# Encoder block on eight cores: the gating unit's mixing moved into the next FFN, attention with longer lags, constants, staging loads and final multiply re-timed

## The chip, the cores and the metric

The kernel runs on the 8 cores of one Trainium2 chip, each core with one of 8 sequences. The time is the device time of the slowest core in microseconds (us). Some executions fall in a slow state, in which one die, sometimes both, runs at a lower granted clock (the share of full speed that the throttle gave the matmul engine) and takes some per cent longer, whatever the kernel is.

## The reference, cut to what matters

```python
x = x + 0.5 * swiglu(rmsnorm(x, norm_ffn1), w_gate, w_up, w_down)     # FFN 1
h = rmsnorm(x, norm_mix)
z = h @ w_in                      # q, k, v | u, v_s | two gates
y_att = chunked_rel_attention(q, k, v, rel_bias)     # 64-frame chunks, 9-chunk key band, 8 heads
y_sgu = spatial_gating(gelu(z_sgu), ...)             # layer norm, 128x128 mixing per group, times u
merged = g_att * (y_att @ w_branch_att) + g_sgu * (y_sgu @ w_branch_sgu)
x = x + merged @ w_out
x = x + 0.5 * swiglu(rmsnorm(x, norm_ffn2), ...)     # FFN 2
return rmsnorm(x, norm_final)
```

Per core x is 4096 x 1024, the FFN width is 2816.

## The kernel before

A sequence is worked in 8 tiles of 512 frames. For tile t the order on the matmul engine (PE) is: FFN 1 of tile t+1 with attention of tile t interleaved, merge and output projection of tile t, input projections of tile t+1 ("win"), FFN 2 of tile t. Engines run their instructions in program order, and a helper adds the semaphore waits. Weights come through six slots of 1 MB. At first use a chunk is loaded as float32 and cast by a software DMA issued from POOL; some uses later it is written back as bfloat16, and from then on loaded by a plain DMA from SP.

An FFN is a generator of 60 "pieces": 44 gate and up pieces of 8 matmuls, then 16 down pieces of 11. `hooks` maps a piece to work that is put behind it.

```python
for f2 in range(NFC // 2):                       # 11 weight chunks
    sl, k = get_slot(("ffs", i, f2))
    for a in range(2):
        ...  # 8 matmuls into bank bg; ACT: tanh or silu -> TG; (tanh: DVE multiplies by bank bg)
        hook(); yield
        ...  # 8 matmuls into bank bu; DVE: HT[fc] = bank bu * TG   (L469)
        if a == 1: free_slot(k)                  # allows the load of the chunk six ahead
        hook(); yield
```

The start, as DVE and the POOL queue see it (cut):

```python
...  # sp: G3, then GF, BG, LNG, LNB, BSB; pool: IDB, then six weight chunks; act: X of tile 0
p.add("dve", memset NHALF, QBD, VR, PB)
... # four norms of tile 0
def late_consts():
    p.dma("pool", RB); p.dma("pool", WST)        # behind the six chunks in the same queue
    p.add("dve", memset of part of WST)          # waits for the WST load   (L346)
    p.add("dve", BG *= 0.5)
```

The mixing at the end of the projections, and one attention step:

```python
for s in range(4):                               # sgu_mix, in banks 4 and 5
    b = 4 + s % 2
    ...  # 8 small matmuls (L603); DVE: + BSB -> TG (L608), * UT -> YS
# attention: scores(i) | transp(i-1) | pv(i-2), 34 steps
def scores(i):
    ...  # PE scores; DVE add bias, row minimum; ACT exp
    p.add("dve", reciprocal of the row sum)      # waits for ACT   (L662)
    p.add("dve", probabilities *= reciprocal)    # (L664)
```

The norms and the final norm:

```python
def norm_stats(t, which, s):
    if which == 0 and t >= 2: p.dma("sp", XS[s % 2] <- x)
    p.add("act", square with row sum); rsqrt on POOL
    p.add("act", XN = x * rsqrt)                 # waits for POOL
def final(t, s):
    p.add("act", square with row sum); rsqrt on POOL
    p.add("dve", X = X * rsqrt * GF)             # waits for POOL   (L773)
```

## Time and profile before

| | before |
|---|---|
| time, median of the first 3 runs | 3028.04 us (3026.66 to 3031.44) |
| span of the slowest core in the profile | 3025.5 us |
| PE busy | 2854.2 us, so 171 us idle |
| first FFN matmul, first projection matmul | 27.1 us, 192.1 us |
| FFN 2 of tile 0 from, to | 467.5 us, 589.6 us |

A line of a wait table reads "who <- who ended it: us in total, times, longest". A timeline line reads "start, duration, engine, line, operation, out<-in, count, [idle before <- releaser]". In the slices every digit is the busy share of 1/40 of the span in tenths. In a table by stage each engine (PE, its weight load PEld, DVE, ACT, POOL, in this order) has its busy time and number of instructions; the last three columns are granted PE clock, DMA share (busy share of the 16 DMA engines; it can read a little over 1) and GB/s. The lines on which the argument stands are in the prediction below. An attention start in the timeline of the kernel before:

```profile
1338.31 1.28 ACT L658 ACT_TABLE_LOAD   x1 [3.38 <-DVE ASTAT L651]
1341.36 0.69 PE L674 MATMUL ps<-IDB,PB 128*128 128x128 bf16 x5 [2.58 <-DVE PB L664]
```

PE reaches the transposition of the first probabilities before they are scaled and stands 2.58 us.

### The profile page before, as it was taken

Reading aid. Unit: us, or ns where it says so; the run is one execution under the profiler, and the core shown is the slowest. Engines: PE = TensorE matmul, PEld = TensorE weight load, DVE = VectorE, ACT = ScalarE, POOL = GpSimd, SP = SyncE. Lnnn points to the kernel's source line nnn. Section 1 sums busy time; section 2 is a strip of 40 time slices with the busy share of each in tenths; the row PEclk is TensorE's granted clock in tenths of the full one; section 3 lists DMA queues with packets and bytes.
Section 4 is the critical chain, followed back from the end, with each engine's and each line's share of the span. In section 5 each row is a group of like instructions: output and inputs, shape, how many; then the busy total and the mean of one; then the engine's idle time right before and its main releaser. Section 6 shows DMA issues by size and latency. Waiting matters only on the chain.

```text
span 3025.5 us, 44880 instructions; the slowest of 8 cores (3003.3 to 3025.5 us)
## 1 busy us (share of the span) xinstructions
PE 2854.2 (94%) x15680; PEld 1387.6 (46%) x15680; DVE 1271.2 (42%) x2457; ACT 1017.5 (34%) x1784; POOL 181.5 (6%) x424
## 2 busy tenths in 40 slices
PE   2999999999989999999999999999999999999998
PEld 1444444455434554445544454444544445445444
DVE  1236443364423644246441464425544255456322
ACT  1223332244312443224332243323433244434221
POOL 1110111100100001000000000000000000000000
PEclk7999999999999999999999999999999999999999
DMA  9987799876876446754344444345343452433432
GB/s 202 170 179 168 142 202 198 201 216 143 220 163 198 164 120 201 194 181 161 133 140 162 156 143 148 131 160 167 132 154 140 157 193 100 163 114 104 167 139 91
DMA packets 103436, 485.37 MB, mean 160 GB/s; under 512 B 9008, under 2 KB 9520, under 8 KB 85936
## 3 DMA queue, kind: packets, MB, share of 16 engines
q1 hardware_dynamic: 82352, 384.35, 36.8%
q0 software_dynamic: 20288, 96.05, 19.7%
q8 instruction: 131, 2.15, 0.3%
q10 hardware_dynamic: 576, 2.10, 0.2%
q14 instruction: 89, 0.73, 0.1%
HBM read 513.50 MB, written 65.01 MB: 191 GB/s over the span
## 4 chain that ended last, share of the span: by engine, by line
PE 79%; DVE 6%; DMA 5%; issue 4%; ACT 2%; another core or an unknown queue 2%; POOL 1%; DVEq 0%; ACTq 0%; POOLq 0%; SPq 0%
PE ps L486 18%; PE ps L448 17%; PE ps L465 17%; PE ps L716 7%; PE ps L523 4%; PE ps L727 4%; PE ps L748 3%; PE ps L509 2%; DMA XS<-x 2%; PE ps L674 2%; PE ps L686 2%; PE ps L413 1%; POOL STAT L369 1%; DVE SC L651 1%
## 5 line engine op out<-in xcount | busy, mean ns | idle before, releaser
L465 PE MATMUL ps<-XT,SLOT 128*128 128x512 bf16 x2816 | 681.0, 386 | 38.6 <-DVE HT L469 38.6
L448 PE MATMUL ps<-XT,SLOT 128*128 128x512 bf16 x2816 | 685.6, 388 | 14.9 <-ACT TG L459 11.7
L486 PE MATMUL ps<-SLOT,HT 128*128 128x512 bf16 x2816 | 636.0, 380 | 2.2 <-DMA SLOT<-wd 2.2
L469 DVE TENSOR_TENSOR HT<-ps,TG 128x512 bf16<-128x512 f32 x352 | 242.0, 690 | 511.3 <-PE ps L465 417.9
L465 PEld LDWEIGHTS ps<-XT,SLOT 128*128 128x128 bf16 x2816 | 271.7, 99 | 348.2 <-issue 61.4
L448 PEld LDWEIGHTS ps<-XT,SLOT 128*128 128x128 bf16 x2816 | 274.4, 99 | 329.8 <-issue 44.8
L486 PEld LDWEIGHTS ps<-SLOT,HT 128*128 128x128 bf16 x2816 | 270.4, 98 | 301.5 <-issue 4.3
L658 ACT ACTIVATE PB<-SC,ASTAT 128x576 bf16<-128x576 f32 (+7 forms) x256 | 190.4, 744 | 478.1 <-DVE ASTAT L651 478.0
L459 ACT ACTIVATE TG<-ps 128x512 f32<-128x512 f32 x176 | 103.7, 594 | 420.8 <-PE ps L448 420.8
L716 PE MATMUL ps<-XT,SLOT 128*128 128x512 bf16 x1024 | 243.6, 381 | 0.0
L651 DVE CUSTOM_DVE_ANT_0 SC<-ps,RB 128x576 f32<-128x576 f32 (+7 forms) x256 | 182.3, 712 | 30.9 <-PE ps L646 28.8
L492 DVE SCALAR_TENSOR_TENSOR X<-ps,X 128x512 f32<-128x512 f32 x128 | 88.4, 690 | 220.2 <-PE ps L486 216.9
L677 ACT ACTIVATE PTS<-ps 128x640 bf16<-128x640 bf16 (+4 forms) x256 | 167.4, 654 | 28.6 <-PE ps L674 27.7
L662 DVE RECIPROCAL ASTAT<-ASTAT 128x1 f32<-128x1 f32 x256 | 41.9, 164 | 315.1 <-ACT PB L658 315.1
L509 PE MATMUL ps<-XT,SLOT 128*128 128x512 bf16 x768 | 168.4, 379 | 0.0
L721 ACT ACTIVATE TG<-ps,BG 128x512 f32<-128x512 f32 x128 | 87.1, 686 | 232.8 <-PE ps L716 232.8
L417 DVE TENSOR_TENSOR XT<-ps,G 128x1024 bf16<-128x1024 bf16 x96 | 116.8, 1219 | 114.0 <-PE ps L413 114.0
L731 DVE SCALAR_TENSOR_TENSOR TG<-TG,ps 128x512 f32<-128x512 f32 x128 | 87.4, 687 | 178.8 <-PE ps L727 150.0
L716 PEld LDWEIGHTS ps<-XT,SLOT 128*128 128x128 bf16 x1024 | 99.1, 98 | 113.6 <-issue 2.4
L455 DVE SCALAR_TENSOR_TENSOR TG<-TG,ps 128x512 f32<-128x512 f32 x176 | 120.6, 685 | 48.0 <-ACT TG L453 40.7
L367 POOL TENSOR_SCALAR STAT<-STAT 128x1 f32<-128x1 f32 x128 | 24.3, 189 | 1825.0 <-ACT XN L397 1392.5
L674 PE MATMUL ps<-IDB,PB 128*128 128x128 bf16 x1200 | 109.4, 220 | 25.6 <-DVE PB L664 24.4
(73 smaller groups left out, 2352.5 us busy)
## 6 DMA issues: line engine op xcount, KB each, us to landing
SLOT<-ffs SPq DMA_DIRECT2D x133, 1024.0 KB, 5.7
SLOT<-wds SPq DMA_DIRECT2D x48, 1024.0 KB, 4.9
SLOT<-fsrc POOLq DMA_DIRECT2D x43, 1024.0 KB, 13.2
SLOT<-mgs SPq DMA_DIRECT2D x47, 768.0 KB, 5.4
SLOT<-wis SPq DMA_DIRECT2D x31, 1024.0 KB, 5.8
ffs<-SLOT SPq DMA_DIRECT2D x22, 1024.0 KB, 10.0
SLOT<-wds SPq DMA_DIRECT2D x24, 768.0 KB, 4.7
SLOT<-wd POOLq DMA_DIRECT2D x16, 1024.0 KB, 14.1
```

Of the source, the lines that this page charges most:

```text
L448: p.add("pe", lambda e, kc=kc, W=W, bg=bg: e.matmul(bank(bg), lhsT=W[:, kc * 128:(kc + 1) * 128], rhs=xt[:, kc, :], start=(kc == 0), stop= ...
L465: p.add("pe", lambda e, kc=kc, W=W, bu=bu: e.matmul(bank(bu), lhsT=W[:, 1024 + kc * 128:1024 + (kc + 1) * 128], rhs=xt[:, kc, :], start=(k ...
L469: p.add("dve", lambda e, buf=buf, bu=bu, fc=fc: e.tensor_tensor(out=HT[:, fc, :], in0=bank(bu), in1=buf[:], op=ALU.mult), reads=[rb(bu), b ...
L486: p.add("pe", lambda e, fc=fc, W=W, by=by, s=s: e.matmul(bank(by), lhsT=HT[:, fc, s * 128:(s + 1) * 128], rhs=W, start=(fc == 0), stop=(fc ...
L509: p.add("pe", lambda e, kc=kc, W=W, b=b, cc=cc: e.matmul(bank(b), lhsT=W[:, kc * 512 + cc * 128:kc * 512 + (cc + 1) * 128], rhs=XT[t % 2][ ...
L523: p.add("pe", lambda e, kc=kc, W=W, b=b, s=s: e.matmul(bank(b), lhsT=XT[t % 2][:, kc, s * 128:(s + 1) * 128], rhs=W[:, kc * 512:(kc + 1) * ...
L651: p.add("dve", lambda e: e.tensor_tensor_reduce(out=sc[:, 0:nb], in0=S2[:, 512 - n_prev * 64:512 + n_cur * 64], in1=RB[:, hp, j0:576], sca ...
L658: p.add("act", lambda e: e.activation(out=pbuf[:, off + j0:off + 576], in_=sc[:, 0:nb], func=AF.Exp, bias=ASTAT[:, a0:a0 + 1], scale=-1.0, ...
L674: p.add("pe", lambda e, kt=kt: e.transpose(out=pt[:, kt * 128:(kt + 1) * 128], in_=pbuf[:, kt * 128:(kt + 1) * 128], identity=IDB[:]), rea ...
L677: p.add("act", lambda e: e.activation(out=PTS[i % 2][:, kt0 * 128:640], in_=pt[:, kt0 * 128:640], func=AF.Copy), reads=[rb(6)], writes=[(" ...
L716: p.add("pe", lambda e, kc=kc, W=W, bgt=bgt, j=j: e.matmul(bank(bgt), lhsT=W[:, j * 1024 + kc * 128:j * 1024 + (kc + 1) * 128], rhs=XT[par ...
L727: p.add("pe", lambda e, c4=c4, W=W, bbr=bbr, j=j, Y=Y: e.matmul(bank(bbr), lhsT=W[:, 2048 + j * 512 + c4 * 128:2048 + j * 512 + (c4 + 1) * ...
```

## The change

The intent is to fill PE's gaps. The core of the diff:

```diff
-            p.dma("sp", G3); p.dma("pool", IDB)          # ahead of X
+            p.dma("act", TG[0] <- ident); p.dma("act", G3)   # behind X (now half on sp); DVE casts the identity
-            (memsets of QBD, VR, PB and the WST memset at the front of DVE)
+            add_hook(hk, 6, const_loads)                 # pieces of the first FFN
+            add_hook(hk, 40, const_ops)
...
-                for f2 in range(NFC // 2):
+                for f2 in (3, 8, 9, 10, 2, 0, 1, 4, 5, 6, 7):
...
-                (mixing behind the projections, banks 4 and 5)
+            def sgu_hooks(hk, t):
+                for s in range(4):
+                    add_hook(hk, 3 + 3 * s, P(sgu_mix, t, s))   # in the next FFN, bank = dense_bank()
...
-            N_ATT = 3 * 34
+            N_ATT = 4 * 35
-                    for fn, i in ((scores, step), (transp, step - 1), (pv, step - 2)):
+                    for fn, i in ((scores, step), (normal, step - 1), (transp, step - 2), (pv, step - 3)):
...
-            norm_stats: XS load, square, root, scaling in one place
+            norm_sq, norm_cp: the scaling some pieces after the square (on DVE at the start, behind the first FFN and in the last merge)
+                    add_hook(hk, 12, P(load_xs, t + 2, 0), P(load_xs, t + 2, 1))
+            (XS of s = 2, 3 loaded right behind the scaling of s = 0, 1)
...
+                    if s:
+                        add_hook(hk, down(1, s), P(final_mul, t, s - 1))   # one step after the root
```

The new order of chunks keeps the parts of HT that hold the mixing's operands (0 to 3 and 8 to 15) unwritten until the fourth piece of mixing is done.

## The prediction

> **What bounds the kernel now.** I read the page's busy shares and 40 slices first, then who waited for whom on the matmul engine, then the timeline around its long gaps, and last the engines' shares by stage.
>
> ```profile
> PE 2854.2 (94%) x15680; PEld 1387.6 (46%) x15680; DVE 1271.2 (42%) x2457; ACT 1017.5 (34%) x1784; POOL 181.5 (6%) x424
> PE   2999999999989999999999999999999999999998
> DMA  9987799876876446754344444345343452433432
> q1 hardware_dynamic: 82352, 384.35, 36.8%
> q0 software_dynamic: 20288, 96.05, 19.7%
> ```
>
> PE is the bound in all but the first slice; DVE and ACT are far from full. The work of PE doesn't change, so only its idle time (3025.5 - 2854.2 = 171 us) and time at a low clock can be won. DMA is near full in the early slices. Per MB of destination, the casting software queue costs 0.197 x 3025.5 / 96.05 = 6.2 us and the hardware queue 0.368 x 3025.5 / 384.35 = 2.9 us.
>
> ```profile
> PE ps L603 <- DVE TG L608: 39.1, 16, 4.2
> PE ps L465 <- DVE HT L469: 38.6, 1, 38.6
> PE ps L674 <- DVE PB L664: 24.4, 26, 2.9
> PE ps L413 <- ACT XN L402: 17.9, 7, 4.9
> PE ps L448 <- ACT TG L459: 11.7, 4, 8.0
> ```
>
> Two waits dominate: the gating unit's mixing (L603), 4.9 us in each of 8 tiles, and one single wait of 38.6 us at the start. The timeline says what that one is:
>
> ```profile
> 75.90 0.48 DVE L346 MEMSET WST<- 64x512 bf16 x1 [48.94 <-DMA WST<-wst]
> 76.48 1.28 DVE L469 TENSOR_TENSOR HT<-ps,TG 128x512 bf16<-128x512 f32 x2
> 77.31 3.47 PE ps L465 x8
> ```
>
> (The third line is from the chain of work that ended last.) DVE runs in order. The memset of WST waits for a load behind six weight chunks in the same queue, and the evictions that PE needs stand behind it.
>
> The low clock comes with the gaps. After a mixing stage:
>
> ```profile
> 1211.34 0.64 PE L603 MATMUL ps<-WST,HT 128*64 128x128 bf16 x8 [4.19 <-DVE TG L608]
> 1213.37 3.59 PE L448 MATMUL ps<-XT,SLOT 128*128 128x512 bf16 x8
> 1218.70 1.89 PE L448 MATMUL ps<-XT,SLOT 128*128 128x512 bf16 x8
> ```
>
> Eight matmuls take 3.59 us instead of 1.89. Summing all start-to-start times of 512-column matmuls between 0.3 and 0.5 us, less the usual 0.216, gives 43 us: 16 after the eight mixing stages, 11 after six attention starts, the rest at the start, at the end and after DMA waits.
>
> ```profile
> 27.00:39.00 12.00, 11.57 (x40) 4.50 (x40) 0.00 (x0) 1.42 (x3) 0.00 (x0) 1.00 1.03 234
> 39.00:77.00 38.00, 0.00 (x0) 0.00 (x0) 1.09 (x3) 0.37 (x1) 0.70 (x1) 0.55 1.03 197
> 77.00:146.00 69.00, 68.69 (x311) 30.82 (x312) 13.90 (x21) 18.09 (x29) 7.86 (x15) 0.97 0.91 169
> 235.00:372.00 137.00, 136.04 (x752) 66.18 (x752) 70.75 (x201) 53.37 (x133) 10.52 (x21) 0.98 0.76 162
> 467.00:583.00 116.00, 112.70 (x538) 51.67 (x539) 28.51 (x38) 25.34 (x39) 11.75 (x24) 0.97 1.02 210
> ```
>
> The last two columns are DMA share and GB/s. DMA is full while PE stands still at 39 to 77 us, and full again in the second half of the first tile.
>
> **What the Trainium skill says.** "TensorE: Matmul & The Clock Gate", section "What's actually happening": an idle window of about 3.4 us puts the array back to half clock and a similar busy window brings it back. The trace agrees: gaps of 3.9 us and more are followed by 8 to 14 matmuls 0.43 us apart; gaps of about 1 us are not. "DMA: Bandwidth & Descriptors", section "Issuing engines are not separate DMA queues": loads issued from several engines share the same 16 DMA engines. The share of 1.03 in 27 to 77 us with three issuers agrees; moving X and the constants between queues buys order, not bandwidth. "ScalarE: Activation LUTs", section "What ACT_TABLE_LOAD costs": about 1283 ns per load; the trace has 1.28 us.
>
> **The change part by part.**
>
> (a) Start. Memsets and constants leave the front; the wait on WST leaves DVE (memsets at piece 40 of the first FFN), so PE's 38.6 us plus 1.6 us of low clock go. The four norms are pipelined, with their scaling on DVE; the first matmul should move from 27 to about 20 us, another 7 us. But those 47 us aren't free: DMA was full in that time. The work that must land before the first FFN is done: 11 gate/up chunks x 6.5 us (1.05 MB x 6.2) = 72; down weights 4 x 6.5 + 2 x 4.9 = 36; X for two tiles, 4.2 MB x 2.9 = 12; constants about 9; six write-backs x 3 = 18. Sum about 147 us. The last down chunk then lands at about 149 to 158 us instead of 160, and from it some 16 us of matmuls remain: the first FFN ends at 165 to 175 us instead of 187.5. Gain 18 us of the 47; the rest turns into waits for weights. The memsets at piece 40 (3.47 + 3.47 + 2.62 us and two small ones, 10 us of DVE) may cost 2 us, hidden in the same waits.
>
> (b) Mixing in pieces in the next FFN. The 32 small matmuls per tile stay, but each group of 8 stands among dense ones, with a dense bank. Per tile the two gaps (about 3.9 + 1.0 us) and about 2 us of low clock go: 7 us. This needs the new order of weight chunks, so that HT 0..3 and 8..15 are still whole; that costs nothing. For tiles 2 to 6 this is 5 x 7 = 35 us. Tiles 0 and 7 start an FFN with attention beside it, so the layer norm chain (DVE ends it about 4 us after the last projection matmul) delays the first score evictions and about half of the gain stays a wait: 3 to 4 us each. Tile 1's gain falls into the full-DMA stage at 467 to 583 us, where a weight wait of 2.25 us is already seen: 1 us.
>
> (c) Attention with one more step between exp and transposition. The reciprocal no longer blocks DVE (315 us of DVE idle before L662), but PE lost only 24 us to this, most of it as one gap per tile at the start of each FFN with attention: 0.66 + 2.58 us, plus about 1.9 us of low clock. At that place DVE still does the last tile's final multiply, ACT still loads the exp table (1.28 us), and the next tanh stands behind the first exp, so, replayed with the durations of the start at 1332 us, the second score eviction ends at about 1342.2 us while PE wants those banks for the third scores at 1339.9. By this working 2.5 us of gap stay in place of 3.2 and the low clock shrinks: 1.5 us x 6 = 9 us. The small gaps elsewhere in attention (ten of 0.3 to 0.6, and 0.73, 1.39, 1.27) go: 7 us.
>
> (d) Staging loads. ACT waited 118.6 us for XS; PE lost 8.01 + 0.98 + 1.09 + 1.60 us = 11.7 to it and 1.6 to the low clock. XS now loads at least 6 pieces (10 us) ahead against landings of 5.5 to 10 us in later tiles and 20 us in tile 1: 12.5 us.
>
> (e) Final multiply one step later. It takes a 2.5 us wait from DVE 32 times; PE sees it before the last merge (3.55 us, and 2.7 of low clock): 5 us. The drain at the end, last matmul to last store, stays at about 17 us. The norm gaps at 187.5 and 2895 us (3.8 and 4.8 us) keep their chain of eviction, square, root, scaling and transposition, so stay.
>
> Sum: 18 (a) + 35 + 4 + 4 + 1 (b) + 9 + 7 (c) + 12.5 (d) + 5 (e) = 95.5 us. 3028 - 96 = 2932 us.
>
> **The rivals.** First: the start is not DMA-limited and the whole 47 us comes through. For it: PE waits for no weight in the first 500 us of the trace. Against: at 39 to 77 us DMA share is 1.03 with PE idle, and each chunk lands about 9.5 us after the one before, against 6.9 us of matmuls. It would give about 2905. Second: attention's first gap vanishes as intended, 31 us instead of 9: about 2910; both together 2880. Third: the added pieces make DVE late where attention runs (DVE 70.75 of 137 us there), mixing adds 1.4 us of DVE per piece, banks come free late, and gaps of a microsecond appear at each piece; or ACT or POOL wait in order for a norm and stop the FFN as in (d). Shares near one half speak against it; it would give 2960 or so. Fourth: early tiles, with DMA full, return nothing: (a) and the first tiles' (b) fall to 5 us, 2950.
>
> **Range and chances.** 2932 us, 8 in 10 between 2890 and 2962. The threshold of 2% is at 2967.5, a gain of 60.5 us. The parts that rest on plain removal of a seen gap ((b) for tiles 2 to 6, (d), (e) and the small gaps: 35 + 12.5 + 5 + 7 = 59.5) reach it almost alone. Faster 0.91, within 2% 0.08, slower 0.01.
>
> **What would show it.** (a) The wait for L469 gone, waits of L448 or L486 for DMA of SLOT in the first 180 us in its place, the first FFN ending at 165 to 175 us. (b) No wait at the mixing matmuls over 1 us, no run of 0.43 us matmuls at the start of FFN 2 in tiles 2 to 6, a period per tile of some 358 instead of 368 us. (c) At each attention start a wait of scores for the eviction before them, about 2 us. (d) ACT's wait for XS near zero. The prediction is wrong if PE's idle time stays over 120 us, if the first FFN ends before 155 or after 185 us, or if new waits for DVE or ACT appear in every tile.

## The result, and the profile after

The two fast runs of the changed kernel took 2917.69 and 2916.78 us; two more runs fell in the slow state (2969 and 3158 us). The ratio of the fast runs is 0.9632, 95% interval 0.9604 to 0.966: 3.7% faster. A ratio is the mean time of one kernel's fast runs over that of the other's in the same rounds, so it isn't quite the ratio of the medians. Experiments compare with 2917 us, the middle of the two.

The page of the changed kernel, its slowest core with a span of 2916.1 us:

```profile
PE 2825.4 (97%) x15680; PEld 1381.4 (47%) x15680; DVE 1265.9 (43%) x2470; ACT 1005.9 (34%) x1772; POOL 181.0 (6%) x423
PE   6799999899999999999999999999999999999998
```

PE's idle time fell from 171 to 91 us, and its busy time by 29 us with the same number of matmuls. The latter is low clock: the start-to-start times of 512-column matmuls between 0.3 and 0.5 us, less 0.216 each, sum to 26 us instead of 43; these sums don't explain the other 12 us (the ends of matmuls are modelled). Slices 1 and 2, where PE had stood still, read 6 and 7 instead of 2 and 9. Who PE waited for now (line numbers shift with every edit: L603, L642, L465 and L486 of the kernel before are L622, L661, L483 and L504 here):

```profile
PE ps L430 <- DVE XN L417: 33.1, 8, 19.2
PE ps L661 <- DVE ASTAT L685: 15.4, 8, 2.1
PE ps L504 <- DMA SLOT<-wd: 12.3, 4, 6.0
PE ps L466 <- DMA SLOT<-fsrc: 12.2, 2, 11.8
```

The mixing's 39.1 us and the 38.6 us at the start are gone. In place of the second stand waits for weights, one of them 11.8 us long (at 82.7 us). L430 is the norms' transposition, L661 the score matmuls of an attention start (the third scores at six of them, 2.13 us each).

Where the time came from, by the first matmul of a stage in both traces:

| stage begins | before, us | after, us | earlier by, us |
|---|---|---|---|
| FFN 1 of tile 0, up | 27.1 | 32.3 | -5.1 |
| its down matmuls | 146.2 | 124.7 | 21.5 |
| projections of tile 0 | 192.1 | 177.1 | 15.0 |
| FFN 1 of tile 1 | 235.6 | 213.9 | 21.6 |
| FFN 2 of tile 0 | 467.5 | 439.4 | 28.1 |
| FFN 1 of tile 2 | 589.6 | 570.2 | 19.4 |
| FFN 1 of tile 3 | 965.3 | 925.4 | 39.9 |
| FFN 1 of tile 6 | 2068.5 | 1991.3 | 77.2 |
| FFN 2 of tile 7, up | 2900.8 | 2792.3 | 108.5 |
| end | 3025.5 | 2916.1 | 109.4 |

Tile 0's up matmuls win 26.6 us (from -5.1 to 21.5), and the stages with the first two mixings 6.6 and 6.5, but 15 us are lost again by 570 us: 6.5 in the first down matmuls and 8.7 in FFN 2 of tile 0. From then on each tile is 11 to 21 us shorter. The table by stage of the changed kernel shows what holds the early part:

```profile
32.30:124.70 92.40, 80.19 (x352) 35.11 (x353) 17.97 (x23) 20.17 (x32) 9.44 (x17) 0.93 1.03 191
124.70:177.10 52.40, 45.40 (x241) 21.48 (x240) 23.24 (x26) 5.99 (x11) 7.53 (x17) 0.91 1.00 181
439.00:570.00 131.00, 122.47 (x595) 55.31 (x594) 35.18 (x49) 27.23 (x42) 15.50 (x31) 0.95 0.97 197
```

DMA is full (1.03, 1.00, 0.97) in all three stages in which PE waits for weights; the second and the third give time back, the first wins less than the 38.6 us of its old wait. But a full DMA alone isn't a loss: its share was 1.00 from 177 to 214 us and from 345 to 439 us too, where PE was busy for 37.0 of 37 and 93.7 of 94 us. The share says where waits can come; the wait table says whether they do.

A piece of mixing among dense matmuls, and the front, in the timeline of the changed kernel:

```profile
1170.19 0.41 PE L622 MATMUL ps<-WST,HT 128*64 128x128 bf16 x8
1170.54 1.90 PE L466 MATMUL ps<-XT,SLOT 128*128 128x512 bf16 x8
...
18.11 0.23 DVE L328 CAST IDB<-TG 128x128 bf16<-128x128 f32 x1 [16.92 <-DMA TG<-ident]
21.43 1.22 DVE L434 TENSOR_TENSOR XT<-ps,G 128x1024 bf16<-128x1024 bf16 x1 [2.33 <-DMA G<-g]
32.25 3.21 PE L466 MATMUL ps<-XT,SLOT 128*128 128x512 bf16 x8 [1.48 <-DVE XT L434]
```

The eight small matmuls cost 0.35 us from start to start of the neighbours, and the next eight run at 1.90 us, so at full clock. At the front the first matmul came later than before: the identity landed at 18 us behind X, and the gains at 21 us.

An attention start in the changed kernel:

```profile
1286.35 1.28 ACT L677 ACT_TABLE_LOAD   x1 [2.81 <-DVE ASTAT L670]
1287.64 0.78 ACT L677 ACTIVATE PB<-SC,ASTAT 128x576 bf16<-128x576 f32 x1
1288.42 0.57 ACT L471 ACTIVATE TG<-ps 128x512 f32<-128x512 f32 x1
1289.16 0.69 DVE L473 SCALAR_TENSOR_TENSOR TG<-TG,ps 128x512 f32<-128x512 f32 x1 [2.29 <-ACT TG L471]
1289.77 0.75 DVE L670 CUSTOM_DVE_ANT_0 SC<-ps,RB 128x576 f32<-128x576 f32 x1
1290.67 0.32 PE L661 MATMUL ps<-KT,QBD 128*128 128x384 bf16 x1 [2.13 <-DVE ASTAT L685]
```

Table load, first exp, tanh of the next piece, its multiplication, eviction of the second scores, third scores: the wait of the transposition has gone, and a wait of the scores of 2.13 us stands in its place.

### The profile page after: what moved, and what is told of

Its sections match the earlier page's. It is cut to its first block, busy times and chain, and to the rows that moved or that the text cites. A ratio compares the mean times of both kernels' runs of the same rounds, so it can differ in the third digit from the quotient of the medians.

```text
span 2916.1 us, 44695 instructions; the slowest of 8 cores (2900.9 to 2916.1 us)
## 1 busy us (share of the span) xinstructions
PE 2825.4 (97%) x15680; PEld 1381.4 (47%) x15680; DVE 1265.9 (43%) x2470; ACT 1005.9 (34%) x1772; POOL 181.0 (6%) x423
## 4 chain that ended last, share of the span: by engine, by line
PE 89%; DMA 6%; DVE 2%; issue 2%; ACT 1%; POOL 0%; DVEq 0%; ACTq 0%; POOLq 0%; SPq 0%
PE ps L504 21%; PE ps L466 19%; PE ps L483 18%; PE ps L739 8%; PE ps L527 5%; PE ps L541 4%; PE ps L750 4%; PE ps L771 3%; DMA SLOT<-fsrc 3%; PE ps L697 2%; PE ps L709 2%; DMA SLOT<-wd 2%; PE ps L430 1%; PE ps L665 1%; PE ps L661 1%
## 5 line engine op out<-in xcount | busy, mean ns | idle before, releaser
L466 PE MATMUL ps<-XT,SLOT 128*128 128x512 bf16 x2816 | 676.4, 384 | 15.2 <-DMA SLOT<-fsrc 12.2
L483 PE MATMUL ps<-XT,SLOT 128*128 128x512 bf16 x2816 | 667.8, 380 | 0.0
L504 PE MATMUL ps<-SLOT,HT 128*128 128x512 bf16 x2816 | 640.8, 382 | 12.3 <-DMA SLOT<-wd 12.3
L504 PEld LDWEIGHTS ps<-SLOT,HT 128*128 128x128 bf16 x2816 | 272.0, 98 | 319.3 <-issue 22.5
L483 PEld LDWEIGHTS ps<-XT,SLOT 128*128 128x128 bf16 x2816 | 270.8, 98 | 298.6 <-issue 4.5
L739 PE MATMUL ps<-XT,SLOT 128*128 128x512 bf16 x1024 | 241.9, 379 | 0.0
L527 PE MATMUL ps<-XT,SLOT 128*128 128x512 bf16 x768 | 168.4, 379 | 0.0
L403 ACT ACTIVATE XN<-X 128x1024 bf16<-128x1024 f32 x72 | 76.1, 1057 | 193.4 <-DVE X L510 87.7
L791 ACT ACTIVATE XN<-X 128x1024 bf16<-128x1024 f32 x32 | 33.9, 1058 | 254.7 <-DVE X L510 254.7
## 6 DMA issues: line engine op xcount, KB each, us to landing
ffs<-SLOT SPq DMA_DIRECT2D x22, 1024.0 KB, 11.9
```

The source lines that it names most:

```text
L466: p.add("pe", lambda e, kc=kc, W=W, bg=bg: e.matmul(bank(bg), lhsT=W[:, kc * 128:(kc + 1) * 128], rhs=xt[:, kc, :], start=(kc == 0), stop= ...
L483: p.add("pe", lambda e, kc=kc, W=W, bu=bu: e.matmul(bank(bu), lhsT=W[:, 1024 + kc * 128:1024 + (kc + 1) * 128], rhs=xt[:, kc, :], start=(k ...
L504: p.add("pe", lambda e, fc=fc, W=W, by=by, s=s: e.matmul(bank(by), lhsT=HT[:, fc, s * 128:(s + 1) * 128], rhs=W, start=(fc == 0), stop=(fc ...
L527: p.add("pe", lambda e, kc=kc, W=W, b=b, cc=cc: e.matmul(bank(b), lhsT=W[:, kc * 512 + cc * 128:kc * 512 + (cc + 1) * 128], rhs=XT[t % 2][ ...
L739: p.add("pe", lambda e, kc=kc, W=W, bgt=bgt, j=j: e.matmul(bank(bgt), lhsT=W[:, j * 1024 + kc * 128:j * 1024 + (kc + 1) * 128], rhs=XT[par ...
```

## The experiments

All kernels gave correct results. Each was timed in 3 rounds beside the kernel before; where I give a time it is the median of the kernel's fast runs. "Trace" means the profiled run's slowest core. A difference from the changed kernel is one of medians taken in different rounds, and the kernel before had fast medians from 3026 to 3032 us in these rounds. By the ratios, which take that drift out, the 18, 9 and 7 us of a_nolag, a_xs_late and a_final_early below become 13, 7 and 5, and the intervals of all three overlap the change's (0.9604 to 0.966). So these three rest on the waits that return in their traces, not on the time alone.

**b_start: the kernel before, only the wait on WST taken out of DVE's front.**

```diff
             def late_consts():
                 p.dma("pool", RB); p.dma("pool", WST)
+            def const_ops():
                 p.add("dve", memset of part of WST)
                 p.add("dve", BG *= 0.5)
+            h0[40] = const_ops
```

> The kernel before, with one edit: the memset of WST and the scaling of BG go to DVE at piece 40 of the first FFN, so that no eviction stands behind the WST load. Theory (DMA-limited start): the 38.6 us wait before the up matmuls goes, waits for weight loads take most of its place, the first FFN ends (first projection matmul) at 170 to 178 us instead of 192, the whole gains 12 to 20 us less what the full-DMA stage of FFN 2 takes back, so 8 to 20 us: about 3010 to 3020. Rival (start limited by the wait alone): 35 to 40 us, about 2990.

Two fast runs, 3013.64 and 3018.84 us, against a mean of 3029.7 us for the four fast runs of the kernel before in these rounds: 13.5 us, too few runs for an interval. In the trace the up matmuls end 26.6 us earlier, the first projection matmul comes at 175.9 us (16.2 us earlier), and FFN 1 of tile 2 at 579.6 (10.0 us earlier). PE's waits up to 180 us in this kernel:

```profile
PE ps L488 <- DMA SLOT<-wd: 7.3, 2, 5.7
PE ps L450 <- DMA SLOT<-fsrc: 7.3, 2, 4.0
```

PE's largest single wait, 38.6 us, was worth 13.5 us, because DMA was full under it. The rival falls.

**a_ident_first: the changed kernel, identity and gains loaded ahead of X.**

```diff
+            p.dma("act", TG[0] <- ident); p.dma("act", G3)
             load_x(0)
-            p.dma("act", TG[0] <- ident); p.dma("act", G3)
```

> The changed kernel with the loads of the identity and the norm gains issued ahead of X. The first FFN matmul should move from 32 to 20 to 23 us in both theories. Theory (DMA-limited start): the first projection matmul stays at 177 us within 3, and the time within 4 us of the changed kernel's 2917. Rival (latency of the front counts): 9 to 12 us less, about 2906.

2918.0 us, ratio 0.963 (0.9602 to 0.9658), so the same as the change. The first matmul came at 26.0 us, 6.3 us earlier and not the 10 us expected (X of the second and fourth sub-tile, behind the identity and the gains on ACT's queue, now landed at 13.8 and 18.9 us), and the first projection matmul at 178.0 instead of 177.1. Six microseconds at the front vanish completely: the front isn't what holds the first FFN.

**a_wb_later: the changed kernel, write-backs of FFN 1's weights one use later.**

```diff
-                        if u >= (first_seen[chunk] * 2) % NREP:
+                        th = (first_seen[chunk] * 2) % NREP
+                        if chunk[:2] in (("ffs", 0), ("wds", 0)):
+                            th = min(2, th + 1)
+                        if u >= th:
```

> The changed kernel with the write-back of converted FFN 1 weights put one use later, so that the first FFN has no write-backs (six of about 3 us of DMA less) and the two next FFN 1 passes have more casting loads. Theory (DMA-limited start): the first projection matmul moves from 177 to 160 to 167 us; the next FFN 1 has DMA time free (0.76 before) and takes the added 39 us of DMA with at most a few us of waits: total 5 to 17 us less than the changed kernel, 2900 to 2912. Rival (start limited by PE and its chains): 177 stays within 3 us and the total stays or gets worse.

One fast run, 2906.57 us, 10.7 us less, beside slow ones only; so no interval. In the trace the first projection matmul comes at 165.2 us, 11.9 us earlier, and 11.1 of it are left at the end. The stages of this kernel's first down matmuls and of FFN 1 of tile 1, and, of its waits over the whole span, those for weights and the one for HT:

```profile
114.20:165.20 51.00, 44.29 (x242) 21.61 (x241) 23.29 (x26) 6.00 (x11) 8.05 (x17) 0.95 0.77 136
200.00:332.00 132.00, 129.88 (x753) 64.10 (x751) 72.36 (x207) 50.67 (x128) 13.94 (x26) 1.00 0.96 175
...
PE ps L507 <- DMA SLOT<-wd: 8.0, 2, 6.7
PE ps L507 <- DVE HT L490: 3.5, 2, 3.3
PE ps L469 <- DMA SLOT<-fsrc: 3.3, 2, 2.4
```

Taking DMA work out of the first FFN, and nothing else, brings its end forward; the next FFN takes that work on with a DMA share of 0.96 and loses nothing. This is the direct sign that the first FFN was held by DMA: its up matmuls (36 to 114 us) now keep PE busy for all of 78.5 us, still at a DMA share of 1.04. The waits for weights that are left are all in FFN 2 of tile 0, which loses 2 us. The edit also uncovers the 10 us of memsets at piece 40: PE now waits 3.3 us for HT.

**a_sgu_after: the changed kernel, mixing behind the projections as before.**

```diff
                 win_cols(t, 1, post_k); h(4)
+                for s in range(4):
+                    sgu_mix(t, s)                # b = 4 + s % 2
-                    add_hook(hk, 3 + 3 * s, P(sgu_mix, t, s))
```

> The changed kernel with the mixing put back after the projections, in banks 4 and 5, all else changed. Theory: two gaps of 4 and 1 us and 2 us of low clock return in each tile, 6 to 7 us in tiles 2 to 6, 3 to 6 in the others: 40 to 50 us slower than the changed kernel, about 2960. Rival (in pieces the mixing costs the FFN something of its own, in DVE time or banks, that this gives back): under 30 us slower.

2957.6 us, ratio 0.9758 (0.9735 to 0.978): 40 us slower. In the trace every FFN behind the mixing starts 6.4 to 7.0 us later. In tile 1 the 6.7 us are given back within the same FFN 2 (7.7 us, as PE then waits less for weights), and in tile 7 2.4 us of them. The wait is the old one:

```profile
PE ps L624 <- DVE TG L629: 39.5, 16, 4.3
```

**a_nolag: the changed kernel, attention in three stages and 34 steps as before** (the body of `normal` back at the end of `scores`).

> The changed kernel with attention as before: reciprocal and scaling right behind the exp of the same step, three stages and 34 steps. Theory (the longer lag took the wait of the first transposition, 2.6 us, and its low clock at six starts, and the small waits of transpositions): 15 to 26 us slower than the changed kernel, about 2937, waits of the transposition for DVE PB back at 20 us or more. Rival (the final multiply put one step later did that, by freeing DVE at the start): under 8 us slower.

2935.4 us, ratio 0.9676 (0.9652 to 0.9699): 18 us slower. The waits of the transposition are back:

```profile
PE ps L693 <- DVE PB L683: 21.4, 11, 2.9
```

By stage it is 5.8 us in FFN 1 of tile 1, 0.2 to 3.7 us in each of the six next (9.7 in sum), and 4.4 us in FFN 2 of tile 6. So half of it lies at the first and the last start, where the kernel before, with its mixing in front, had no such wait (0.1 and 1.3 us of idle PE in the up matmuls there, against waits of 2.2 and 2.5 us for PB here): with the mixing moved, the lag also keeps a new wait away.

**a_final_early: the changed kernel, final multiply right behind its root** (the body of `final_mul` back in `final`).

> The changed kernel with the final multiply issued right behind its root, as before. Theory: DVE waits for POOL 32 times again, the wait before the last merge returns (2.5 us and 2.7 of low clock), and the first scores are evicted about half a microsecond later at six starts: 5 to 10 us slower. Rival (it is what shortened the attention starts): 15 to 25 us slower.

2924.5 us, ratio 0.9649 (0.963 to 0.9668): 7 us slower. In the trace 4.4 us are the end of FFN 2 of tile 6 and 4.3 the last merge; at six attention starts a wait of 0.7 to 0.9 us before the first scores is back, and with the low clock the stages there differ by at most 2.3 us either way. The wait before the last merge:

```profile
2735.36 1.45 PE L750 MATMUL ps<-YA,SLOT 128*128 128x512 bf16 x4 [3.56 <-DVE YA L716]
```

So (c)'s gain is the lag's, not the multiply's: the rival of both runs falls.

**a_xs_late: the changed kernel, each XS load issued with its square.**

```diff
             def norm_sq(t, which, s):
+                if which == 0 and t >= 2:
+                    load_xs(t, s)
-                    add_hook(hk, 12, P(load_xs, t + 2, 0), P(load_xs, t + 2, 1))
```

> The changed kernel with each XS load issued where its square is issued, as before; square and scaling stay split. Theory (the load's landing was the wait): 10 to 18 us slower, of it 8 to 10 in FFN 2 of tile 1 and 1 to 2 in each later one, ACT's wait for XS back at 80 us or more. Rival (the split of square and scaling is what keeps ACT from stopping the FFN): under 5 us slower.

2925.9 us, ratio 0.9655 (0.9637 to 0.9673): 9 us slower, a little under the range expected and over the rival's, so the time doesn't decide between them. ACT waits again:

```profile
ACT XN L405 <- DMA XS<-x: 144.3, 21, 27.1
```

But not where I had said. In the trace (the slowest run, 2932 us) 7 us came in FFN 2 of tile 0, 6.3 in that of tile 2 and none in tile 1. The four fast runs differ by 7 us, and I take it that how much of ACT's wait reaches PE depends on when the load happens to land; that isn't shown, and the place isn't settled.

**a_exp_ahead: the changed kernel, exp table loaded ahead of the attention start.**

```diff
+            def exp_ahead():
+                p.add("act", exp of a 128x1 column)
+                if t < n_tiles - 2:
+                    add_hook(hk, down(0, 2), exp_ahead)   # in FFN 2; for tiles 0 and 7 in win
```

> The changed kernel with one exp of a 128x1 column issued on ACT during the down matmuls ahead of an attention start, so that the exp table (1.28 us) is loaded before the first real exp. Theory (the 2.13 us gap at each start is the chain eviction, table load, exp, tanh, eviction): the gap falls to 0.9 us or less at six starts and takes the 1.4 us of low clock with it: 12 to 18 us less than the changed kernel, about 2902. Rival (DVE's queue sets the gap): the gap stays over 1.5 us, under 5 us less.

2899.5 us, ratio 0.9565 (0.9548 to 0.9581): 18 us less than the change. The same place as above, in this kernel's timeline:

```profile
1279.75 0.78 ACT L677 ACTIVATE PB<-SC,ASTAT 128x576 bf16<-128x576 f32 x1 [2.83 <-DVE ASTAT L670]
1282.78 0.32 PE L661 MATMUL ps<-KT,QBD 128*128 128x384 bf16 x1 [0.85 <-DVE ASTAT L685]
1283.02 1.89 PE L466 MATMUL ps<-XT,SLOT 128*128 128x512 bf16 x8
```

The gap is smaller by just the 1.28 us of the load, and the matmuls behind it run at full clock (1.89 us instead of the 3.45 us that this group took in the changed kernel). Thus 1.28 us of table load were worth 2.6 to 3.2 us at five of the six starts and 1.3 at one.

**a_combo and a_combo2: the helpful edits together.** The first joins the three edits above (identity first, exp table ahead, FFN 1 write-backs later) and spreads the memsets over pieces 12, 16 and 20; the second puts FFN 2's write-backs later as well.

```diff
-                        if chunk[:2] in (("ffs", 0), ("wds", 0)):     # a_combo
+                        if chunk[0] in ("ffs", "wds"):                # a_combo2
```

> The changed kernel with the three helpful edits together (identity and gains first, exp table ahead, FFN 1 write-backs one use later) and the memsets of QBD, VR and PB spread over pieces 12, 16 and 20. Parts: 18 us (exp), 11 (write-backs), 3 (the DVE wait of 3.3 us after piece 40), and, with the first FFN no longer held by DMA, up to 6 for the earlier first matmul: 2880 to 2892 us. If DMA again takes the earlier start back, 2886 to 2892; if not, 2878 to 2883.

> The same with the write-backs of FFN 2's weights one use later as well. Theory (FFN 2 of tile 0 is limited by DMA): its waits of some 10 us and their low clock shrink, and FFN 2 of tiles 1 and 2 takes the added loads within the six slots of prefetch: 3 to 12 us less than the first of the two. Rival (the added casts make FFN 2 of tile 1 DMA-limited, 17 x 6.5 + 18 + 6 = 135 us of DMA in 117): equal or up to 15 us more.

a_combo: 2879.1 us, ratio 0.9518 (0.9497 to 0.9538), inside the range; the first projection matmul comes at 160.8 us. DMA still takes some of it: two waits for chunks at 60 and 83 us and one at 119 us remain. a_combo2: 2875.3 us, ratio 0.9503 (0.9488 to 0.9518). In its trace FFN 2 of tile 0 has no wait for weights left, and FFN 1 of tile 2 begins 11.3 us earlier than in a_combo; but FFN 2 of tile 2 loses 6 us, of it one gap of 4.2 us in the first of these waits; the other two are what stood behind it:

```profile
PE ps L513 <- ACT TG L486: 4.2, 1, 4.2
...
1204.36 0.58 POOL L285 DMA_DIRECT2D SLOT<-wd  x1 [16.89 <-DMA ffs<-SLOT]
1206.06 1.15 ACT L424 ACTIVATE XN<-XS,STAT 128x1024 bf16<-128x1024 f32 x1 [6.61 <-POOL STAT L380]
```

PE waited for an activation of the gate; that stood on ACT behind a norm's scaling, the scaling waited for the root on POOL, and the root stood on POOL behind a casting load that waited 16.9 us for a write-back to leave its slot. This is the third rival of the prediction (ACT or POOL wait in order for a norm and stop the FFN), come true once the casts were moved.

Both beat the changed kernel, the second by 42 us. Their intervals overlap, so the 4 us between the two aren't clear.

## Why the prediction was right, point by point

The time predicted was 2932 us, the fast runs are at 2917, inside the range. The sum was 96 us and the measured gain 111. Of the five parts, measured one by one, (a), (b) and (d) came out smaller than said and (c) and (e) 2 us larger by the medians (not by the ratios), so the parts don't explain that the whole came out larger. PE's idle time fell to 91 us (under the 120 named as a sign of being wrong), no wait of PE at the mixing is left, ACT's wait for XS fell from 118.6 to 1.7 us, and a tile takes about 355 us (358 said, 368 before). The one new wait for DVE in every tile is that of the scores, 1 to 2 us, which was announced.

- **(a) Start, 18 us.** The trace has 15.0 us at the first projection matmul and the first FFN ends at 172.5 us (165 to 175 was said); b_start alone has 16.2 there. The waits for weights are in the place predicted. In a_wb_later the DMA account held in sign and in two thirds of its size: six write-backs are 18 us in it, and 12 came out. One step failed: the first matmul was to move to 20 us and moved to 32, since I looked at the compute chain and not at where the identity and the gains stood in the queue behind X. It cost nothing, by a_ident_first, because DMA held the end.
- **(b) Mixing, 44 us.** 40 us by a_sgu_after; 7 us per tile were said and 6.4 to 7.0 measured. By the stages of a_sgu_after tiles 0 and 7 kept about 5 and 4 us, where 3 to 4 were said; tile 1's gain went into the weight waits as said.
- **(c) Lag, 16 us.** 18 us by a_nolag (13 by the ratio), but the agreement is in part luck: 9.7 us came at the six starts, where 9 were said; of the small gaps, 7 us in the sum, few came back; and 10 us came at the first and last start, which part (c) didn't count. At the six starts 2.5 us of gap were to stay, now ending before the scores; the trace has 2.13 us there, and a_exp_ahead shows that the chain is the one worked out. The rival that they vanish with the lag (31 us) falls.
- **(d) Staging loads, 12.5 us.** 9 us by a_xs_late in the median (7 by the ratio), 14 in its trace. Comparing the traces of before and after, FFN 2 of tile 1 gained 10.0 us as said. That undoing the loads brings the wait back elsewhere suggests that the place is chance. Splitting square and scaling wasn't undone by itself, so its share is open.
- **(e) Final multiply, 5 us.** 7 us by a_final_early (5 by the ratio), at the last merge and the end of the FFN before it.

The parts measured one by one, 13.5 + 40 + 18 + 9 + 7, give 88 of 111 us. b_start is an addition to the kernel before and the others are taken away from the changed one; what overlaps, as the split norms do with (a), (d) and (e), isn't separated by these runs. By stage the surplus over the forecast lies mostly in FFN 1 of tiles 2 to 7, which take 24.7 us less in sum than before; undoing the lag gives back 9.7 of them, and to what the rest belongs is open.

Two statements of the Trainium skill were put to use. "TensorE: Matmul & The Clock Gate", section "What's actually happening", on low clock after idle windows: the mixing's 39 us of gaps, most of it in gaps of 3.9 to 4.2 us, count some 55 with the 16 us of low clock behind them. The attention starts go beyond its window of 3.4 us: gaps of 2.25 to 2.93 us in the kernel before were followed by low clock as well, which the prediction's reading (3.9 us and more against about 1 us) left out, and it is why a_exp_ahead is worth twice its table load. "DMA: Bandwidth & Descriptors", section "Issuing engines are not separate DMA queues": in a_ident_first the identity and the gains landed at 5 and 7 us instead of 18 and 21, and the last X load at 18.9 us instead of 13.8, so order moved between loads.

## What to carry to other kernels

Before a large wait is counted as a gain, look at what else was full under it: here 38.6 us of idle PE stood on a DMA share of 1.03 and were worth 13.5 us, and taking DMA work away gave 11 more. A full DMA alone is no proof of a loss: at a share of 1.00 to 1.04 PE also ran without a wait. For small gaps that repeat, count the low clock behind them, which can double their price, and ask for the first late event in the chain: a table load moved ahead of its first use was worth as much as the longer lag. After a change, read the wait that has taken the old one's place; it is the next edit. And look at what stands in order on the engines that are hardly busy: in a_combo2 a root on POOL behind a load cost PE 4.2 us.

## What the Trainium skill lacked or had wrong

- "TensorE: Matmul & The Clock Gate", section "Why this matters for your kernels", asks for no idle gap over about 3 us. Here one gap of 2.13 us at an attention start was followed by 7 or 8 matmuls 0.43 us apart (1.4 us lost) in five of six cases; gaps of 0.85 us in a_exp_ahead by none. In the kernel before, gaps of 2.25 to 2.93 us (at the attention starts with another 0.66 us just ahead) were followed by 6 to 12 of them.
- The same page, section "Seeing it yourself", says that once three cores of a die run dense matmuls the clock falls to 13/16. With all eight cores dense, the fast runs held a mean clock of 0.988 to 0.993 (0.216 us per 512 columns); only in slow runs did one die fall, to 0.87 to 0.97 in this kernel and to 0.82 at the lowest in all runs. That lowest value is near 13/16; whether the slow state is the page's limit isn't shown.
- "DMA: Bandwidth & Descriptors", section "SWDGE vs HWDGE vs iDMA", says that a cast needs the software queue but not what it costs. By the page of the kernel before, a casting load took 6.2 us of all 16 engines per MB of destination and a plain one 2.9. A casting load reads float32, two bytes for each byte that it writes, so most of the difference may be the bytes read.
- No page says what a wait of PE is worth when the DMA share stands near 1 under it: b_start's 38.6 us gave 13.5.
